# A new order of instructions on every engine of a two-level Strassen-Winograd matmul

## The chip, the core and the metric

The kernel runs on one core of a Trainium2 chip. The metric is device time in microseconds (us) from start to end of one execution, the median of several runs. A core has engines that each work through their own queue of instructions in order: TensorE (PE, matmuls into PSUM), VectorE (DVE), ScalarE (ACT), GpSimd (POOL), and the sync engine's queue (SP), which here issues all DMA transfers. They meet at semaphores: an instruction waits until what it reads has been written, and until what it overwrites has been read.

## What is computed

```python
def setup_inputs():
    B, S, D = 8, 2048, 2048
    return {
        "x": np.random.randn(B, S, D).astype(np.float32),
        "w": np.random.randn(D, D).astype(np.float32),
    }

def reference(x, w):
    cs = np.cumsum(x, axis=1)
    diff = cs - np.concatenate([np.zeros((cs.shape[0], 1, cs.shape[2]), dtype=np.float32), cs[:, :-1, :]], axis=1)
    return np.matmul(diff, w).astype(np.float32)
```

A cumulative sum followed by its differences gives x back, so the work is one matmul: 16384 x 2048 times 2048 x 2048.

## The kernel before, in words

**Tiles.** x is cut into 128 row tiles of 128 x 2048 (1 MB), each loaded as two halves of 512 KB. The first four (`PLAIN = 4`) are multiplied directly in bfloat16 while w, 32 blocks of 512 KB, arrives; these are the `plain.h.r.ko` steps. The other 124 go in groups of four through a Strassen-Winograd scheme in float16, which trades matmuls for sums: a group is two pairs (g and h = g + 2), and from the second group on most products are once more split into seven.

**Stages of a tile** (`role` counts tiles from the group's start). `load` brings a half from memory into one of four staging places. `weigh` (ScalarE, L138) sums its absolute values; `mean` (GpSimd, L157), `scale` (VectorE, L159) and `unit` (GpSimd, L160) turn the sums into a row scale; `narrow` (ScalarE, L170) writes the scaled half as float16; `turn` (SP, L187) is a DMA that transposes it into the place from which TensorE loads it. `load4` to `load7` belong to the next group, `load8` and `load10` to the one after it.

**Products.** `P1`, `P2`, `P5`, `P3` and `P4` are the five products that are split into seven (L554). `P1.0` to `P1.6` are their TensorE steps, four matmuls each; `P1.s1` to `P1.s4` the sums of x that they need (VectorE, `s3` on GpSimd); `in1.Q1`, `in1.Q4`, `in5.t21`, `in3.Q1`, `in3.Q3`, `in4.Q1` sums of w blocks in one shared place `flow` (L520), and `in4.Q3` one that is brought by DMA. Within a product a bank of PSUM is used several times: `P1.first` copies it out after step 0 (ScalarE, L571), `P1.out2` after step 2 and `P1.out4` after step 4, and the step that reuses the bank waits for that copy; `P1.middle` and `P1.last` (VectorE, L520) add the copies in. `S2g T2`, `S2h T2`, `S3g T3`, `S3h T3` are whole products of four steps each (L532).

**Results.** `keep` (ScalarE, L568) scales a bank into one of eight result places, `C11g+P2.g` and the like (VectorE, L579) add further banks, `put` (SP, L587) writes a result out. A result place can be reused by a `keep` only when its `put` has landed.

**Start.** w blocks are cast (`cast w.h.ko`, ScalarE) and their largest value is taken (`max w.h.ko`, VectorE). When all 32 have landed, `max`, `max of all`, `uw` and `uinv` give the scale of w, and `B11`, `B21`, `B12` (VectorE, L415) and `B22` (six on ScalarE, L417) make the float16 blocks of w, eight each. `left over.0` to `.3` (TensorE, L430, 16 matmuls) need B11 and B21. `first x` are quarter loads of the first four tiles, `warm` are matmuls on zeros.

**The order.** The code builds a list of operations with `record(label, engine, ask)`; nothing is issued yet. `emit` sorts the list by a number written out for every label and issues each engine's operations in that order:

```python
        for _, _, engine, ask in sorted(ops, key=when) if places else ops:
            after(engine, ask)
```

where `when` is `period * PERIOD + places[period][label]`, and `places[None]` holds for the periods without a table of their own, 4 to 26. Period 0 is the start with the first group, periods 1 to 30 are the other groups, 31 is the last write. Who computes what, and which buffers are used, is fixed when the list is made; the numbers decide only who stands before whom in each engine's queue. A matmul step, a copy or a sum of one group can so stand among those of the next.

Of the kernel before, what the change touches and what calls it, by code (L numbers as in the profile page):

```python
# [10 lines left out]
def kernel(  # L11
# [33 lines left out]
    PERIOD = 2177  # L45
# [12 lines left out]
    B11, T1, B12, T2, B21, T3, B22, T4 = (  # L58
        [p[:, i // 2, i % 2] for p in pieces] for i in range(8)
    )  # L60
# [4 lines left out]
    uw, uinv, wred = (tiny[:, ds(10 + i, 1)] for i in range(3))  # L65
# [289 lines left out]
    cast = {}  # L355
# [777 lines left out]
    for g in range(PLAIN + 4, END, 4):  # L1133
# [8 lines left out]
            'ones': -4955, 'first x.1.0': -4955, 'numbers': -4941, 'numbers turned': -4926,  # L1142
# [522 lines left out]
```

## Time and profile before

| | us |
|---|---|
| median of 3 runs | 1470.49 (1469.99 to 1476.46) |
| the profiled execution | 1472.2 |
| its span, first to last instruction | 1470.4 |
| TensorE busy in it | 1446.3, 6698 matmuls |
| VectorE busy | 1270.1 |
| ScalarE busy | 1127.1 |
| GpSimd busy | 314.8 |
| transfers of the queue | 366.02 MB, 91.5% of the 16 DMA engines' time |

In the views that follow, a group of instructions is named by its line, engine and operation; `arena<-b` means that it reads PSUM banks and writes the tile `arena`. The time before an instruction in which its engine was idle is put down to the one that released it. A matmul's end is modelled, some 0.16 us after the next one starts, so neighbours overlap and waits look that much shorter.

### The profile page before, as it was taken

What the parts mean: (1) busy time and instruction counts of PE and PEld (TensorE: products, weight loads), DVE (VectorE), ACT (ScalarE), POOL (GpSimd) and SP (SyncE); (2) the same over time, 40 slices, a digit from 0 to 9 for tenths busy, and PEclk for the clock granted to TensorE, in tenths of its full rate; (3) what the DMA queues carried; (4) which work ended last, traced back from release to release, by engine and by line L of the source; (5) the groups of instructions that cost most, each with busy time, mean ns of one, the idle gap of its engine ahead of it and who ended that gap; (6) DMA issues with size and microseconds to landing.
All of it is one profiled execution on the core that took longest, in us unless ns stands there. A gap on an engine that the chain in (4) does not pass through costs nothing.

```text
span 1470.4 us, 20821 instructions
## 1 busy us (share of the span) xinstructions
PE 1446.3 (98%) x6698; PEld 652.4 (44%) x6698; DVE 1270.1 (86%) x2075; ACT 1127.1 (77%) x1742; POOL 314.8 (21%) x400
## 2 busy tenths in 40 slices
PE   8999999999999999999999999999999999999998
PEld 3444444444444444444444444444444444444443
DVE  5998898888889888889888889888889888888887
ACT  5996677877787877777877777877777877787773
POOL 0001122222222222222222222212222212212220
PEclk9999999999999999999999999999999999999999
DMA  9999878999889999889999889999899999988983
GB/s 351 353 261 266 220 212 234 256 265 248 236 251 237 266 264 246 238 253 236 267 263 247 242 244 238 270 264 245 235 254 235 270 263 238 251 243 227 261 215 129
DMA packets 348109, 367.34 MB, mean 250 GB/s; under 512 B 271456, under 2 KB 271456, under 8 KB 348000
## 3 DMA queue, kind: packets, MB, share of 16 engines
q1 hardware_dynamic: 348000, 366.02, 91.5%
q8 instruction: 52, 0.85, 0.3%
q14 instruction: 57, 0.47, 0.1%
HBM read 166.20 MB, written 134.74 MB: 205 GB/s over the span
## 4 chain that ended last, share of the span: by engine, by line
PE 87%; DMA 7%; ACT 3%; DVE 2%; issue 1%; SPq 1%; POOL 0%; DVEq 0%; ACTq 0%; POOLq 0%
PE b L554 54%; PE b L532 30%; DMA F<-in_x_dram 3%; PE b L302 2%; DMA W<-in_w_dram 2%; DMA x<-F 1%; ACT arena L568 1%; ACT F L170 1%; DVE arena L520 1%; ACT waste L138 1%; DVE arena L579 1%; DMA W<-in_x_dram 1%; ACT b L571 0%; DMA out_dram<-arena 0%; ACT arena L571 0%
## 5 line engine op out<-in xcount | busy, mean ns | idle before, releaser
L579 DVE SCALAR_TENSOR_TENSOR arena<-b,tiny,arena 128x512 f32<-128x512 f32 x612 | 444.7, 746 | 85.9 <-ACT arena L568 44.5
L532 PE MATMUL b<-W,x 128*128 128x512 f16 x2176 | 515.9, 379 | 0.0
L554 PEld LDWEIGHTS <-arena 128*128 128x128 f16 x2700 | 263.5, 98 | 330.5 <-issue 15.1
L554 PE MATMUL b<-W,arena 128*128 128x512 f16 x1640 | 399.3, 379 | 3.5 <-ACT b L571 2.1
L568 ACT ACTIVATE arena<-b,tiny 128x512 f32<-128x512 f32 x496 | 321.8, 688 | 46.4 <-PE b L532 18.3
L532 PEld LDWEIGHTS <-x 128*128 128x128 f16 x2176 | 212.7, 98 | 256.9 <-DVE x L520 0.2
L170 ACT ACTIVATE F<-F,tiny 128x1024 f16<-128x1024 f32 x246 | 282.6, 1149 | 47.8 <-DVE tiny L159 45.3
L554 PE MATMUL b<-W,x 128*128 128x512 f16 x1180 | 297.8, 379 | 3.4 <-ACT b L571 2.4
L138 ACT ACTIVATE waste<-F 128x1024 uint8<-128x1024 f32 x246 | 260.4, 1059 | 26.9 <-DMA F<-in_x_dram 25.0
L554 PE MATMUL b<-arena 128*128 128x512 f16 x1060 | 271.1, 379 | 2.5 <-ACT arena L568 1.9
L520 POOL TENSOR_TENSOR arena<-x,x 128x512 f16<-128x512 f16 x118 | 149.1, 1264 | 575.5 <-PE b L554 552.8
L571 ACT COPY arena<-b 128x512 f32<-128x512 f32 x294 | 170.7, 581 | 99.2 <-PE b L554 89.9
L554 PEld LDWEIGHTS <-x 128*128 128x128 f16 x1416 | 138.4, 98 | 173.2 <-issue 6.9
L520 DVE TENSOR_TENSOR b<-b,arena 128x512 f32<-128x512 f32 x294 | 204.0, 694 | 12.8 <-ACT arena L571 12.1
L520 DVE TENSOR_TENSOR arena<-W 128x2048 f16<-128x2048 f16 (+1 forms) x127 | 151.4, 1192 | 11.6 <-PE b L554 11.6
L571 ACT COPY b<-b 128x512 f32<-128x512 f32 x147 | 85.1, 579 | 97.6 <-PE b L554 94.0
L157 POOL TENSOR_SCALAR tiny<-tiny 128x1 f32<-128x1 f32 x124 | 68.3, 551 | 383.6 <-ACT waste L138 358.2
L520 DVE TENSOR_TENSOR x<-x,x 128x1024 f16<-128x1024 f16 x124 | 85.3, 688 | 2.0
L520 DVE TENSOR_TENSOR arena<-W,arena 128x2048 f16<-128x2048 f16 (+1 forms) x70 | 76.0, 1085 | 2.1 <-PE b L554 1.7
L520 DVE TENSOR_TENSOR arena<-x,arena 128x512 f16<-128x512 f16 x118 | 49.8, 422 | 32.2 <-PE b L554 28.8
L160 POOL TENSOR_SCALAR tiny<-tiny 128x1 f32<-128x1 f32 x124 | 63.6, 520 | 2.9
L554 PE MATMUL b<-arena,x 128*128 128x512 f16 x236 | 60.6, 379 | 1.4 <-DMA F<-in_x_dram 1.2
(46 smaller groups left out, 627.3 us busy)
## 6 DMA issues: line engine op xcount, KB each, us to landing
F<-in_x_dram SPq DMA_DIRECT2D x246, 512.0 KB, 5.1
out_dram<-arena SPq DMA_DIRECT2D x240, 512.0 KB, 5.5
W<-in_w_dram SPq DMA_DIRECT2D x32, 512.0 KB, 9.8
arena<-kept SPq DMA_DIRECT2D x29, 512.0 KB, 4.5
out_dram<-arena SPq DMA_DIRECT2D x32, 256.0 KB, 3.2
W<-in_x_dram SPq DMA_DIRECT2D x16, 256.0 KB, 7.8
x<-F SPq DMA_TRANSPOSE x246, 4.5
arena<-in_x_dram SPq DMA_DIRECT2D x2, 512.0 KB, 4.1
```

The source lines that it names most:

```text
L138: lambda: nc.scalar.activation(waste, data, ABS, scale=1.0 / ROW, accum_out=m),
L157: lambda: nc.gpsimd.tensor_scalar(m, m2[:, :1], m2[:, 1:], TINY, ADD, MAX),
L160: record(f"unit{role(t)}", "pool", lambda: nc.gpsimd.tensor_scalar(u, m, uw, None, MUL))
L170: lambda: nc.scalar.activation(to, data, COPY, scale=s),
L302: said = nc.tensor.matmul(to[n], xP[:, r, ko, :], b[:, ds(n * NB, NB)], start=(ko == 0), stop=(ko == KO - 1),)
L520: record(label, engine, lambda: on.tensor_tensor(dst, p, q, op))
L532: said = nc.tensor.matmul(to[n], a[k], b[k][:, n, :], start=(start and k == 0), stop=(k == KH - 1), skip_group_check=True,)
L554: said = nc.tensor.matmul(to, a[k], b[k], start=(start and k == 0), stop=(k == 3), skip_group_check=True)
L568: record(label, "act", lambda: nc.scalar.activation(c, p, COPY, scale=u))
L571: record(label, "act", lambda: nc.scalar.copy(to, p))
L579: label, "dve", lambda: nc.vector.scalar_tensor_tensor(c, p, u, c, MUL, ADD)
```

## The change

The numbers in every table of `places`, and `PERIOD`, are others. The list of operations, their engines, operands and buffers are the same. The core of the diff:

```diff
-    PERIOD = 2177
+    PERIOD = 2168
...
-            'ones': -4955, 'first x.1.0': -4955, 'numbers': -4941, 'numbers turned': -4926,
+            'ones': -4948, 'numbers': -4947, 'numbers turned': -4946, 'zeros': -4945,
+            'first x.0.2': -4944, 'eye': -4909, 'first x.0.3': -4889, 'warm.0': -4870,
+            'w.0.0': -4858, 'warm.1': -4844, 'first x.0.1': -4840, 'first x.0.0': -4835,
...
         None: {
-            'P1.0': -1178, 'P1.first': -1134, 'P4.last': -1128, 'P1.1': -1067, 'C21h+P4.h.0': -1054,
-            'P1.s3': -987, 'P1.2': -951, 'P2.0': -949, 'P1.out2': -948, 'P1.s4': -927,
...
+            'P1.0': -1211, 'P1.first': -1149, 'P1.2': -1064, 'P1.s4': -999, 'P4.last': -994,
+            'P1.1': -983, 'P1.out2': -978, 'P1.s3': -955, 'P2.0': -933, 'C21h+P4.h.1': -911,
```

Sorted, the repeated period (4 to 26) reads as follows; a minus sign marks an operation of the period before.

```
TensorE, before:
P1.0 P1.1 -P4.6 P1.2 P2.0 P1.3 P2.1 P1.4 P2.3 P2.2 P1.5 P1.6 P2.4 P2.5 P5.0 P2.6 S2gT2 S2gT2
S2gT2 P5.3 P5.1 P5.2 S2gT2 P5.4 P5.5 P5.6 S2hT2 S2hT2 P3.1 S2hT2 P3.0 S2hT2 P3.2 P3.3 P3.4 P3.5
P3.6 S3gT3 P4.0 P4.1 S3gT3 S3gT3 S3hT3 P4.2 S3hT3 P4.3 S3gT3 S3hT3 S3hT3 P4.4 P4.5
TensorE, after:
P1.0 -P4.4 -S3hT3 -S3hT3 P1.2 -P4.6 P1.1 P2.0 P1.3 P1.4 P2.3 P2.1 P2.2 P1.5 P2.4 P1.6 P2.5 P2.6
P5.0 S2gT2 S2gT2 P5.3 P5.1 P5.2 S2gT2 P5.4 S2gT2 P5.5 P5.6 S2hT2 S2hT2 S2hT2 P3.1 P3.0 S2hT2
P3.2 P3.3 P3.4 P3.5 P3.6 S3gT3 P4.1 S3gT3 P4.0 S3gT3 S3gT3 P4.2 S3hT3 P4.3 P4.5 S3hT3
ScalarE, before:
P1.first -weigh7.0 -weigh7.1 P1.out2 P2.first -narrow7.0 P1.out4 -narrow7.1 C11g.0 P2.out2
weigh4.0 P2.out4 C11g.1 weigh4.1 C11h.0 narrow4.0 P5.first C11h.1 narrow4.1 weigh6.0 P5.out2
weigh6.1 P5.out4 C22g.0 C12g.1 C22h.0 C22g.1 C12g.0 narrow6.0 C12h.0 narrow6.1 P3.first C22h.1
C12h.1 P3.out2 P3.out4 P4.first weigh5.0 weigh5.1 narrow5.0 narrow5.1 P4.out2 C21g.0 C21h.0
C21g.1 P4.out4 C21h.1
ScalarE, after (C11g.0 and the like are keep C11g.0):
P1.first -C21h.1 -weigh7.0 P1.out2 -weigh7.1 P2.first -narrow7.0 -narrow7.1 C11g.0 P2.out2
P1.out4 C11g.1 P2.out4 weigh4.0 weigh4.1 C11h.0 C11h.1 P5.first narrow4.0 narrow4.1 C22g.0
P5.out2 weigh6.0 P5.out4 weigh6.1 C22g.1 narrow6.0 C12g.1 narrow6.1 C12g.0 C22h.0 C12h.0
P3.first C12h.1 C22h.1 P3.out2 P3.out4 weigh5.0 weigh5.1 narrow5.0 P4.first P4.out2 narrow5.1
C21g.0 C21g.1 C21h.0 P4.out4
VectorE, first third, before:
P4.last -C21g+P4.g.1 -P2.s1 -C21g+P4.g.0 C21h+P4.h.0 P1.s4 -P2.s2 in1.Q4 -scale7 S1g P1.middle
C21h+P4.h.1 P2.s4 S3g P2.middle C11g+P2.g.0 S2g in5.t21 C11g+P2.g.1 P1.last scale4
VectorE, first third, after:
P1.s4 P4.last C21h+P4.h.1 C21h+P4.h.0 -scale7 in1.Q4 P1.middle S1g C11g+P2.g.0 P2.middle P2.s4
P1.last S3g in5.t21 S2g C11g+P2.g.1 scale4
SP, before:
load6.1 put-1.0 put0.0 put2.0 turn4.0 load5.0 load5.1 turn6.0 turn4.1 turn6.1 put0.1 in4.Q3
put2.1 load7.0 load7.1 turn5.0 turn5.1 load8.0 put1.1 put1.0 load8.1 put3.1 turn7.0 turn7.1 load10.0
SP, after:
load6.1 put-1.0 put0.0 put2.0 turn4.0 load5.0 load5.1 turn6.0 turn4.1 turn6.1 put0.1 in4.Q3
put2.1 turn5.0 load7.0 load7.1 turn5.1 put1.0 put1.1 load8.0 load8.1 put3.1 turn7.0 turn7.1 load10.0
```

The parts of the other periods that the prediction speaks of (the number before a colon is the period that an operation belongs to):

```
SP at the start, before: first x.1.0 x.0.0 x.1.1 x.0.3 x.0.1 x.0.2 w.0.2 w.0.0 w.0.1 ...
SP at the start, after:  first x.0.2 x.0.3 w.0.0 first x.0.1 x.0.0 w.0.3 first x.1.1 x.1.0 ...
VectorE after uinv, before: B11.5 B21.1 B11.3 B11.2 B21.0 B11.6 B11.0 B21.2 B21.4 B11.1 scale0
  B11.4 B21.7 B11.7 B21.3 B21.5 B21.6 scale2
VectorE after uinv, after:  B21.3 B21.0 B11.1 B11.7 B12.0 B11.0 B21.6 B11.2 B11.6 B11.3 scale0
  B11.5 B11.4 B21.2 scale2 B21.7 B21.1 B21.5 B21.4
period 1, ScalarE, before: ... weigh6.1 C12g.0 C22g.1 C12h.1 C12h.0 narrow6.0 ...
period 1, ScalarE, after:  ... narrow4.1 C12g.1 C22g.1 weigh6.0 weigh6.1 C12g.0 narrow6.0 ...
period 2, TensorE, before: P2.1 P1.0 P2.0 P1.3 P2.2 P1.2 ...
period 2, TensorE, after:  P1.0 1:S3hT3 1:S3hT3 P2.0 1:P4h.0.1 P2.1 P1.2 P1.3 P2.2 ...
period 2, ScalarE, before: ... weigh4.1 weigh6.0 C11g.1 P1.out4 weigh6.1 C11h.1 ...
period 2, ScalarE, after:  ... weigh4.1 C11g.1 P1.out4 weigh6.0 narrow4.0 C11h.0 ...
period 3, TensorE, before: P1.0 P1.1 2:P4.6 P1.2 P2.0 P1.3 P2.3 ...
period 3, TensorE, after:  P1.0 2:P4.4 2:P4.5 2:S3hT3 P1.1 P1.2 2:P4.6 P2.1 P1.3 P2.0 P1.4 P2.3 ...
period 27, ScalarE, before: ... weigh6.0 P5.first weigh6.1 P5.out2 narrow4.1 ...
period 27, ScalarE, after:  ... P5.first weigh6.0 narrow4.1 P5.out2 weigh6.1 ...
period 28, ScalarE, before: ... C11h.0 narrow4.1 weigh6.0 P5.first C11h.1 ...
period 28, ScalarE, after:  ... C11h.0 weigh4.1 P5.first narrow4.0 weigh6.0 P5.out2 ...
period 29, ScalarE, before: ... C11h.1 weigh4.0 weigh4.1 weigh6.0 P5.first weigh6.1 ...
period 29, ScalarE, after:  ... P2.out4 C11g.1 P5.first weigh4.0 P5.out2 weigh4.1 ...
```

More of the change, by code (lines that the diff above doesn't have):

```diff
@@ L1141 @@
         0: {
-            'ones': -4955, 'first x.1.0': -4955, 'numbers': -4941, 'numbers turned': -4926,
[70 rows of a table removed]
-            'max': -2094, 'weigh0.0': -2088, 'max of all': -2086, 'uw': -2069, 'uinv': -2061,
[77 rows of a table removed]
-        },
[48 rows of a table removed]
-        },
[41 rows of a table removed]
-        },
[41 rows of a table removed]
+            'ones': -4948, 'numbers': -4947, 'numbers turned': -4946, 'zeros': -4945,
[69 rows of a table added]
+            'cast w.1.12': -2142, 'max w.1.12': -2142, 'max': -2076, 'max of all': -2059,
[25 rows of a table added]
+            'B12.5': -1259, 'out': -1248, 'narrow1.0': -1229, 'put out': -1210,
[52 rows of a table added]
+        },
[48 rows of a table added]
+        },
[42 rows of a table added]
+        },
[42 rows of a table added]
         },
         27: {
[41 rows of a table removed]
[41 rows of a table added]
         },
         28: {
[40 rows of a table removed]
[41 rows of a table added]
         },
         29: {
[40 rows of a table removed]
[40 rows of a table added]
         },
         30: {
[32 rows of a table removed]
[32 rows of a table added]
         },
         31: {
-            'P4.last': -1221, 'C21h+P4.h.1': -1110, 'C21h+P4.h.0': -1078, 'put-1.0.1': -1068,
-            'put-1.0.0': -1020,
+            'P4.last': -1181, 'C21h+P4.h.1': -1065, 'C21h+P4.h.0': -1031, 'put-1.0.1': -1021,
+            'put-1.0.0': -989,
         },
         None: {
[41 rows of a table removed]
[40 rows of a table added]
         },
```

931 rows, old and new, of the table places are left out of this document.

## The prediction

> **What bounds the kernel now.** I read the busy lines of the page first, then the stretch table, then what TensorE waited for, and last the order of time around single waits.
>
> ```profile
> PE 1446.3 (98%) x6698; PEld 652.4 (44%) x6698; DVE 1270.1 (86%) x2075; ACT 1127.1 (77%) x1742; POOL 314.8 (21%) x400
> ```
>
> TensorE is busy nearly always, and the change leaves its 6698 matmuls alone, so only the time between them can go. The stretch table (length; for each engine busy us and its instructions; clock; DMA share; GB/s) shows where that time lies:
>
> ```profile
> 0.00:19.54 19.54, 12.52 (x58) 5.69 (x59) 8.58 (x16) 6.63 (x7) 0.19 (x4) 0.91 0.89 309
> 42.00:135.00 93.00, 93.00 (x432) 42.12 (x431) 88.28 (x152) 76.78 (x108) 9.59 (x18) 1.00 0.99 294
> 135.00:300.00 165.00, 158.43 (x724) 70.28 (x723) 139.93 (x240) 120.18 (x187) 37.64 (x43) 1.00 0.88 231
> 300.00:1290.00 990.00, 989.90 (x4577) 447.10 (x4576) 866.48 (x1415) 786.69 (x1235) 230.69 (x291) 1.00 0.94 252
> 1290.00:1430.00 140.00, 135.24 (x621) 60.41 (x619) 117.71 (x191) 104.51 (x166) 33.22 (x41) 1.00 0.87 233
> 1465.50:1470.40 4.90, 0.00 (x0) 0.00 (x0) 1.30 (x2) 0.35 (x1) 0.00 (x0) 0.98 0.59 209
> ```
>
> One step of four matmuls takes 0.864 us when nothing is waited for (the starts 559.13 to 560.86 quoted further down), 0.216 a matmul. Against that rate 135 to 300 lacks 165/0.2157 - 724 = 41 matmuls, 8.8 us; 1290 to 1430 lacks 28, 6.0 us; 300 to 1290 lacks 12.7, 2.7 us over 22 groups. 42 to 135 lacks nothing. With the start and the 4.9 us after the last matmul that is all there is: 17.5 us of waits in three stretches. What ended TensorE's waits (total, times, longest), first for 135 to 300, then for 1290 to the end:
>
> ```profile
> PE b L554 <- ACT b L571: 1.9, 2, 1.4
> PE b L554 <- ACT arena L568: 1.9, 2, 1.1
> PE b L554 <- DMA F<-in_x_dram: 1.2, 1, 1.2
> PE b L532 <- DVE arena L520: 0.7, 1, 0.7
> PE b L554 <- DVE arena L520: 0.4, 1, 0.4
> PE b L554 <- ACT arena L571: 0.2, 1, 0.2
> ...
> PE b L554 <- ACT b L571: 3.0, 4, 1.6
> PE b L554 <- ACT arena L571: 1.3, 2, 1.1
> PE b L554 <- DVE arena L579: 0.4, 1, 0.4
> ```
>
> These sum to 6.3 and 4.7 us, less than 8.8 and 6.0: the ends of matmuls are modelled later than their successors start, so each wait shows some 0.16 short. I scale by 1.4 and 1.28. Most are copies out of PSUM on ScalarE, and what held them is seen at two places (start, length, engine, operation, idle before):
>
> ```profile
> 146.57 1.06 ACT L138 ACTIVATE waste<-F 128x1024 uint8<-128x1024 f32 x1 [0.50 <-DMA F<-in_x_dram]
> 147.62 2.40 ACT L568 ACTIVATE arena<-b,tiny 128x512 f32<-128x512 f32 x4
> 148.92 1.02 PE L554 MATMUL b<-arena 128*128 128x512 f16 x4 [0.80 <-ACT arena L568]
> ...
> 1345.20 1.04 ACT L138 ACTIVATE waste<-F 128x1024 uint8<-128x1024 f32 x1
> 1346.24 0.58 ACT L571 COPY b<-b 128x512 f32<-128x512 f32 x1
> 1346.88 1.02 PE L554 MATMUL b<-W,arena 128*128 128x512 f16 x4 [1.64 <-ACT b L571]
> ```
>
> ScalarE takes its instructions in order. A weigh (L138) stands in the queue for a tile that is still landing, or simply ahead of the copy, and the copy that TensorE needs comes behind it.
>
> **The change, part by part.** Nothing is added or removed; every cost is a matter of who stands behind whom.
>
> *135 to 300 (periods 1 to 4), -5.0.* In period 1 keep C22g.1 now comes before weigh6.0 and weigh6.1, so the wait at 148.92 loses its cause. In period 2 TensorE gets five more steps between P1.0 and P1.3 (two of period 1's S3h T3, its P4h.0.1, then P2.1 and P1.2), 4.3 us, which covers the 1.4 us that the copy P1.first was late; P1.out4 moves ahead of weigh6.0. In period 3 P2.3 moves five steps (4.3 us) back, past the late weigh7.1. I count all of the 1.9 behind L571, half of the 1.9 behind L568 (in period 4 keep C22g.1 still follows weigh6.1, with one TensorE step more of cover), half of the 1.1 behind VectorE and the 0.2 as gone: 3.6 x 1.4 = 5.0. The 1.2 stays: it is keep C11h.0, which still stands ahead of P2.out4. Bounds: 2 to 8.
>
> *1290 to 1430 (periods 27 to 30), -3.0.* In periods 28 and 29 P5.first moves ahead of weigh6.0, in 29 ahead of weigh4.0 too, so of the 3.0 behind L571 the 1.64 quoted and about 0.5 go; in 27 weigh6.1 moves behind P5.out2 and P5.4 behind two more steps, so the 0.3 at P5.4 goes. In 29 narrow5.0 and narrow5.1 still precede keep C21h.1 and P4.out4 (1.1 us), which I leave. 2.4 x 1.28 = 3.0; bounds 1 to 5.
>
> *300 to 1290 (the repeated order), -1.5.* One wait recurs here in every period:
>
> ```profile
> 557.31 1.03 PE L554 MATMUL b<-W,x 128*128 128x512 f16 x4
> 558.17 1.03 PE L532 MATMUL b<-W,x 128*128 128x512 f16 x4
> 559.13 1.02 PE L554 MATMUL b<-W,arena 128*128 128x512 f16 x4
> 559.99 1.03 PE L554 MATMUL b<-W,x 128*128 128x512 f16 x4
> 560.86 1.03 PE L554 MATMUL b<-arena 128*128 128x512 f16 x4
> ...
> 557.43 1.16 ACT L170 ACTIVATE F<-F,tiny 128x1024 f16<-128x1024 f32 x1
> 558.47 0.61 ACT L571 COPY b<-b 128x512 f32<-128x512 f32 x1
> ...
> L138 ACT ACTIVATION_READ_ACCUMULATOR waste<-F 128x1 f32 x246 | 47.5, 193 | 0.0
> ```
>
> P3.0 starts at 557.31, its copy P3.first only at 558.47, right behind narrow6.1; P3.2 follows at 559.13, 0.96 after the step between instead of 0.86. In the new order three short copies stand ahead of P3.first, narrow6.1 before them. By the rows, a weigh or a narrow takes ScalarE 1.05 and a copy 0.5 to 0.58 from one start to the next, and a weigh's sum is out 1.25 after its start (0.19 more, the last row); from P5.4's end P5.out4, weigh6.1 and a wait for mean6 and scale6 make 2.4 us, then two narrows and four copies 4.4: free at 6.8, while eight TensorE steps end at 6.9. I take 0.07 of the 0.10, times 22: 1.5. The rest of the period I walked the same way. P5.first now stands ahead of narrow4.0, with two TensorE steps as cover instead of three, 0.5 us to spare. P2.out2 has one step as cover instead of two; with its copy free to start that suffices, as one step suffices elsewhere in this period. The tightest is VectorE. scale7 now stands early in its queue and holds it until weigh7.1 and mean7 are done. From P1.0's start, the last S3h T3 of the period before ends at 3.7; then come keep C21h.1, weigh7.0, P1.out2 and weigh7.1 (0.58 + 1.05 + 0.5 + 1.25), and mean7: 7.4 us. Behind scale7 stand in1.Q4, P1.middle, S1g, C11g+P2.g.0, P2.middle and more up to S2g, some 7 us of VectorE work with holds for P2.out2 and for P1.6 in it, so that S2g ends at 16.0. Step 19, S2g T2.0.0, starts at 16.4: about 0.3 to spare, if mean7 is short. It can be either:
>
> ```profile
> 535.51 1.52 POOL L157 TENSOR_SCALAR tiny<-tiny 128x1 f32<-128x1 f32 x1 [0.89 <-ACT waste L138]
> 535.74 1.22 DVE L520 TENSOR_TENSOR arena<-W,arena 128x2048 f16<-128x2048 f16 x1
> 545.13 0.30 POOL L157 TENSOR_SCALAR tiny<-tiny 128x1 f32<-128x1 f32 x1 [6.00 <-ACT waste L138]
> ```
>
> The long one ran beside in1.Q4, the short one beside a sum in PSUM. In the new order in1.Q4 stands behind scale7, which waits for mean7, so VectorE is idle then: I take 0.30. At 1.52 P2.4 would be late by about 0.25 a period, 5.5 us in all. Bounds of this part: -2.7 to +5.5.
>
> The Trainium skill, SBUF — State Buffer, "Who interferes with whom", has it that GpSimd and a VectorE instruction with two SBUF inputs exclude each other for a whole instruction; the two rows agree, and by that rule the 5.5 us do not come.
>
> *0 to 135, +0.2.* The first w block is asked for third instead of eighth, so the first real matmuls come earlier; but the transfers fill this stretch (DMA share 0.89, then 0.99), and its end hangs on VectorE:
>
> ```profile
> 63.26 6.72 DVE L415 TENSOR_SCALAR W<-W,tiny 128x1024 f16<-128x1024 f32 x10
> 70.29 4.05 DVE L415 TENSOR_SCALAR W<-W,tiny 128x1024 f16<-128x1024 f32 x6
> 72.01 3.62 PE L430 MATMUL b<-W,arena 128*128 128x512 f16 x16
> ```
>
> The last four of these 16 matmuls start at 74.60 (72.01 + 12 x 0.216), 0.26 after the sixteenth block of B11 and B21 ends (70.29 + 4.05). The new order puts B12.0 among them, so it is the seventeenth: 0.67 later, less 0.26, less what TensorE finds to do meanwhile. Bounds -0.7 (blocks ready sooner) to +1.7, from the clock:
>
> ```profile
> 12.72:16.13 3.41, 1.44 (x6) 0.58 (x6) 1.22 (x1) 2.56 (x3) 0.00 (x0) 1.00 1.03 410
> 16.13:19.54 3.41, 3.41 (x15) 1.75 (x14) 1.70 (x2) 2.79 (x4) 0.00 (x0) 0.50 1.05 408
> ```
>
> After a stretch with TensorE mostly idle the granted clock is 0.50 for 3.41 us, which costs half of it, 1.7. The new order's first matmuls are as gappy, so I expect one such stretch again.
>
> The Trainium skill, TensorE: Matmul & The Clock Gate, "Part 1: The HAM clock gate (the "warmup" mystery)", says the gate judges windows of 3413 ns; the rows agree. By it a second idle window would make the start term +1.9 instead of +0.2.
>
> *New waits, +1.5.* No trace shows the new order's own. Bounds: none, to as much as the old order has in its eight special periods, 8.8 + 6.0 = 14.8. I take a tenth, since the order that repeats (2.7 us in 22 periods) is nearer to what a settled order has.
>
> **Sum:** -5.0 - 3.0 - 1.5 + 0.2 + 1.5 = -7.8. The profiled execution took 1472.2 (span 1470.4), so 1464.4 for it; the median of the runs is 1470.5, 1.7 below, so the forecast is 1462.7.
>
> **The rivals.** *Nearly all waits go:* 1470.5 - 17.5 = 1453. For it: nearly all have one cause, a weigh or a landing ahead of a copy. Against: a write-back's landing and two narrows still stand ahead of copies. *The waits move:* the special periods have as many as before at other places, and only 1.5 to 2 us of the loop are won: 1468.5. For it: VectorE at 88.28 of 93 us in 42 to 135 leaves no room to give. *Slower, by one landing:* put2.1 must have landed before keep C21h.0 reuses its buffer. In the loop put2.1 waits for C12h+Y.1, behind P3.6, which is now TensorE's fortieth step of the period instead of the thirty-seventh; so it goes out some 2.1 us closer to that copy, and the copy stands ahead of P4.out4 and P1.first, which P4.6 and P1.2 wait for.
>
> ```profile
> out_dram<-arena SPq DMA_DIRECT2D x240, 512.0 KB, 5.5
> ...
> 1343.58 0.69 ACT L568 ACTIVATE arena<-b,tiny 128x512 f32<-128x512 f32 x1 [2.12 <-DMA out_dram<-arena]
> ```
>
> The median landing is 5.5 us and about 7 would still do; ScalarE has been held 2.12 by such a landing. If it held TensorE by 0.8 in each of 22 periods, that is +17.6 in place of the loop's -1.5: -6.3 + 17.6 = +11.3, 1481.8. From 0.3 a period on (6.3/22) the kernel is slower than before. Against it: no row shows a wait of this kind between 300 and 1290, and the loads of the loop get more room: weigh6.1 starts about 1 us after load6.1's landing in the old order and, by the same walk, some 3 us after it in the new.
>
> **How the numbers follow.** Forecast 0.49 (own range 1458 to 1467), nearly all waits go 0.20, the waits move 0.18, slower 0.13. A measurement tells 0.5%, 7.4 us, from no change: below 1463.1 is faster, above 1477.8 slower. Over half of the forecast's chance (0.28) and all of the second's are faster: 0.48. The rest of the forecast's and the third's are 0.39 within, and 0.13 slower. The range leaves out half of the slower rival and part of the second: 1454 to 1474.
>
> **What would show it.** Right: between 300 and 1290 TensorE has 4580 or more matmuls in 990 us; 135 to 300 has over 740; no copy behind a weigh that waits for a landing; one stretch at clock 0.50. Wrong: a wait that recurs every 44 us, on keep C21h.0, S2g or P2.out2, or a B block that ends later than 75 us.

## The result, and the profile after

The new order takes 1459.65 us (median of 4 runs, 1458.38 to 1461.24) where the old takes 1471.76 (4 runs, 1469.99 to 1476.46): 0.9913 of the time, with a 95% interval of 0.9887 to 0.994. The forecast was 1462.7. The profiled execution took 1459.5, its span is 1457.7, 12.7 less than before.

The busy lines of the new kernel, and its stretch table (length; for each engine busy us and its instructions; clock; DMA share; GB/s):

```profile
PE 1440.2 (99%) x6692; PEld 652.4 (45%) x6698; DVE 1245.1 (85%) x2075; ACT 1132.1 (78%) x1742; POOL 288.1 (20%) x400
```

```profile
0.00:19.54 19.54, 12.90 (x75) 6.39 (x77) 9.73 (x18) 7.71 (x8) 0.19 (x4) 1.00 0.89 312
42.00:135.00 93.00, 89.49 (x412) 40.15 (x413) 85.52 (x149) 73.81 (x102) 9.04 (x18) 1.00 0.99 289
135.00:300.00 165.00, 164.16 (x759) 74.02 (x758) 143.69 (x249) 125.78 (x196) 35.25 (x45) 1.00 0.89 242
300.00:1290.00 990.00, 989.70 (x4585) 448.39 (x4584) 846.22 (x1418) 793.09 (x1238) 208.28 (x292) 1.00 0.91 251
1290.00:1430.00 140.00, 140.00 (x647) 63.20 (x646) 123.08 (x200) 103.61 (x165) 32.00 (x39) 1.00 0.85 234
1453.00:1457.70 4.70, 0.00 (x0) 0.00 (x0) 0.73 (x2) 0.00 (x0) 0.00 (x0) 0.79 0.59 193
```

Six records of matmuls are missing in this trace, all before 68 us (the weight loads, x6698, are complete). From 135 on the table shows 35, 8 and 26 matmuls more than before in the same stretches. From 42 to 135 it shows 20 fewer, 17 without the missing records: here the new order waits where the old one did not. What ended TensorE's waits between 42 and 135 (total, times, longest), which was an empty list before, then between 135 and 300:

```profile
PE b L532 <- DVE arena L520: 2.3, 1, 2.3
PE b L532 <- DMA x<-F: 0.6, 1, 0.6
PE b L430 <- DVE W L415: 0.5, 1, 0.5
```

```profile
PE b L554 <- ACT arena L571: 0.6, 1, 0.6
PE b L554 <- DVE arena L579: 0.2, 1, 0.2
```

Since both kernels run the same steps, the loss can be set down for each part of the list: the time from a part's first matmul to that of the next part, less its matmuls at 0.2157 us (the rounding of this rate alone is worth 0.2 us in the column 5-26). All kernels of this study in one table (us; "plain" are the bfloat16 steps, "group 0" the first group; the runs behind the first two come below):

| | before the first step | plain | group 0 | groups 1-4 | 5-26 | 27-30 | last step to end | median of runs |
|---|---|---|---|---|---|---|---|---|
| before | 14.4 | 2.7 | 0.0 | 9.3 | 3.2 | 6.6 | 5.3 | 1471.76 |
| after | 12.3 | 2.3 | 4.0 | 1.7 | 0.95 | 1.2 | 6.1 | 1459.65 |
| e1, ten moves on ScalarE | 14.0 | 1.6 | 0.9 | 7.3 | 5.8 | 7.1 | 5.3 | 1471.94 |
| e13, nine of them | 14.6 | 1.3 | 0.0 | 5.7 | 7.5 | 6.0 | 5.4 | 1471.17 |
| e2, old start | 14.7 | 0.6 | 6.6 | 6.1 | 0.95 | 1.2 | 6.0 | 1464.95 |
| e3, old end | 11.8 | 3.1 | 4.0 | 2.0 | 0.95 | 11.1 | 5.3 | 1470.74 |
| e11, old ScalarE, VectorE, GpSimd in 2 and 3 | 11.8 | 1.8 | 5.1 | 23.8 | 0.95 | 1.2 | 5.4 | 1481.20 |
| e9, old transfers | 11.4 | 2.8 | 4.1 | 10.0 | 2.1 | 10.6 | 5.9 | 1479.45 |
| e8, new transfers alone | 14.7 | 2.2 | 0.0 | 11.3 | 53.4 | 15.8 | 6.8 | 1532.98 |
| e6, old order, late load | 14.4 | 1.2 | 0.0 | 9.5 | 49.0 | 7.2 | 5.4 | 1516.19 |
| e12, the same, copy ahead | 15.1 | 1.6 | 0.0 | 9.8 | 49.8 | 6.2 | 5.3 | 1520.05 |
| e7, new order, late load | 11.9 | 2.7 | 5.6 | 2.7 | 12.8 | 1.1 | 6.1 | 1474.41 |
| e5, start mended | 11.6 | 3.3 | 3.5 | 1.9 | 0.95 | 1.5 | 5.9 | 1458.91 |
| e10, writes later | 14.4 | 0.2 | 1.1 | 1.9 | 0.95 | 0.5 | 5.9 | 1457.05 |

Before to after: groups 1 to 4 give 7.5, groups 27 to 30 give 5.5, the repeated order 2.2, the start up to the end of the plain steps 2.5; group 0 costs 3.9 and the end 0.8. But for the medians, each row is one execution. The first two columns differ from one to the next also where the table of period 0 is the same: they sum to 15.3 to 17.1 in the seven traces with the old start (16.2 on average) and to 13.6 to 14.9 in the seven with the new (14.5). The trace of the old order is the slowest of its seven, so of the 2.5 at the start about 1.7 is what these traces give to the order.

### The profile page after: what moved, and what is told of

The parts are those of the page before. It is cut to its first block, busy times and chain, and to the rows that moved or that the text cites. A ratio compares the mean times of both kernels' runs of the same rounds, so it can differ in the third digit from the quotient of the medians.

```text
span 1457.7 us, 20733 instructions
## 1 busy us (share of the span) xinstructions
PE 1440.2 (99%) x6692; PEld 652.4 (45%) x6698; DVE 1245.1 (85%) x2075; ACT 1132.1 (78%) x1742; POOL 288.1 (20%) x400
## 4 chain that ended last, share of the span: by engine, by line
PE 92%; DMA 5%; ACT 1%; issue 1%; DVE 0%; SPq 0%; DVEq 0%; POOL 0%; ACTq 0%
PE b L554 60%; PE b L532 32%; DMA W<-in_w_dram 2%; DMA W<-in_x_dram 2%; DMA out_dram<-arena 0%; DMA x<-arena 0%; DMA F<-in_x_dram 0%; ACT waste L138 0%; ACT arena L287 0%; ACT F L170 0%; DVE arena L579 0%; ACT arena L318 0%; ACT arena L568 0%; ACT W L417 0%; SPq L245 0%
## 5 line engine op out<-in xcount | busy, mean ns | idle before, releaser
L579 DVE SCALAR_TENSOR_TENSOR arena<-b,tiny,arena 128x512 f32<-128x512 f32 x612 | 439.7, 743 | 55.4 <-ACT arena L568 42.8
L554 PEld LDWEIGHTS <-arena 128*128 128x128 f16 x2700 | 264.0, 98 | 321.3 <-issue 3.5
L554 PE MATMUL b<-W,arena 128*128 128x512 f16 x1640 | 405.6, 379 | 0.6 <-ACT arena L571 0.6
L568 ACT ACTIVATE arena<-b,tiny 128x512 f32<-128x512 f32 x496 | 322.3, 685 | 51.4 <-PE b L532 39.4
L554 PE MATMUL b<-W,x 128*128 128x512 f16 x1180 | 297.1, 379 | 0.0
L571 ACT COPY arena<-b 128x512 f32<-128x512 f32 x294 | 169.7, 586 | 147.5 <-PE b L554 136.8
L554 PE MATMUL b<-arena 128*128 128x512 f16 x1060 | 266.9, 379 | 0.5 <-DVE tiny L159 0.3
L520 POOL TENSOR_TENSOR arena<-x,x 128x512 f16<-128x512 f16 x118 | 142.7, 1210 | 543.9 <-PE b L554 511.9
L554 PEld LDWEIGHTS <-x 128*128 128x128 f16 x1416 | 138.5, 98 | 167.4 <-issue 0.7
L157 POOL TENSOR_SCALAR tiny<-tiny 128x1 f32<-128x1 f32 x124 | 41.8, 337 | 439.3 <-ACT waste L138 414.3
L571 ACT COPY b<-b 128x512 f32<-128x512 f32 x147 | 85.0, 578 | 35.8 <-DVE arena L579 20.6
L520 DVE TENSOR_TENSOR x<-x,x 128x1024 f16<-128x1024 f16 x124 | 82.3, 681 | 0.2
L160 POOL TENSOR_SCALAR tiny<-tiny 128x1 f32<-128x1 f32 x124 | 72.1, 583 | 0.7
L554 PE MATMUL b<-arena,x 128*128 128x512 f16 x236 | 60.2, 379 | 0.0
```

Of the source, the lines that this page charges most:

```text
L157: lambda: nc.gpsimd.tensor_scalar(m, m2[:, :1], m2[:, 1:], TINY, ADD, MAX),
L160: record(f"unit{role(t)}", "pool", lambda: nc.gpsimd.tensor_scalar(u, m, uw, None, MUL))
L520: record(label, engine, lambda: on.tensor_tensor(dst, p, q, op))
L554: said = nc.tensor.matmul(to, a[k], b[k], start=(start and k == 0), stop=(k == 3), skip_group_check=True)
L568: record(label, "act", lambda: nc.scalar.activation(c, p, COPY, scale=u))
L571: record(label, "act", lambda: nc.scalar.copy(to, p))
```

## The experiments

**Copies ahead of weighs, nothing else (e1, e13).** The prediction read the waits as copies that stand behind a weigh, a narrow or a keep. So the old order got those moves and no others:

```diff
         1: {
-            'keep C22g.1': -133,
+            'keep C22g.1': -175.5,
         2: {
-            'P1.first': -1015, 'P1.out4': -501,
+            'P1.first': -1018.5, 'P1.out4': -538.5,
         3: {
-            'keep C11h.0': -609,
+            'keep C11h.0': -574.5,
         27: {
-            'weigh6.1': -306,
+            'weigh6.1': -231.5,
         28: {
-            'P2.first': -950, 'weigh6.0': -410,
+            'P2.first': -955.5, 'weigh6.0': -266.5,
         29: {
-            'weigh6.0': -425, 'P4.out4': 994,
+            'weigh6.0': -318.5, 'P4.out4': 918.5,
```

In period 1 keep C22g.1 goes ahead of weigh6.1; in 2 P1.first ahead of weigh4.0 and P1.out4 ahead of keep C11g.1; in 3 keep C11h.0 behind P2.out4; in 27 weigh6.1 behind P5.out2; in 28 P2.first ahead of narrow7.1; in 28 and 29 weigh6.0 behind P5.first; in 29 P4.out4 ahead of narrow5.1.

> The old order, with nine instructions of ScalarE's queue at another place in the special periods (1, 2, 3, 27, 28, 29): each copy out of PSUM that a weigh, a narrow or a keep held up goes ahead of it. TensorE, VectorE and SP keep the old order. Theory (the gain comes from copies that no longer stand behind weighs and landings): each moved copy starts when its bank is ready, so of the waits seen in the old trace about 0.97 (period 1), 1.0 and 0.35 (2), 1.34 (3), 0.42 (27), 0.54 and 1.04 (28), 0.5 and 1.2 (29) go, 7.4 in all: about 1464.5, half of what the new order wins. Rival (the new places of TensorE's steps, which cover the waits, do it): the waits come back at the next copy or at the weigh that is late now, and 2 us at most are won: 1470.

Its run held a tenth move, keep C21h.0 of period 28 behind P1.first of 29, by which that keep reads other values and one part of the result differs. It was run again without it:

> The first run again with the nine moves alone: in that run a tenth was in the kernel, keep C21h.0 of period 28 behind P1.first of 29, so that this keep took the bank after the next product's copy had overwritten it and its part of the output was another. Theory now (a copy moved ahead by itself makes the weigh or keep behind it late, and that is needed as soon): no gain, 1470 to 1474. Rival (the tenth move cost what the nine won): 1466 or less.

Measured: 1471.94, ratio 0.9993 (0.9976 to 1.0009), and 1471.17, ratio 0.9991 (0.9978 to 1.0004). No gain. The stretches of e13:

```profile
135.00:300.00 165.00, 161.86 (x741) 72.14 (x741) 144.47 (x246) 123.22 (x193) 37.83 (x45) 1.00 0.87 238
300.00:1290.00 990.00, 987.02 (x4557) 445.40 (x4556) 864.11 (x1408) 783.84 (x1230) 229.81 (x289) 1.00 0.95 250
1290.00:1430.00 140.00, 136.23 (x623) 60.58 (x622) 118.52 (x192) 104.47 (x166) 33.55 (x41) 1.00 0.86 233
```

By the step starts the named waits did go or shrink (0.97 in period 1, 1.34 in 3 and 1.2 in 29 are gone, 1.8 in 28 is 0.2), and 135 to 300 won 17 matmuls. But others appeared behind what is late now: in 27, where weigh6.1 went back, P5.1 and P5.6 lose 1.3 where P5.4 had lost 0.4; in 28 P2.4 and P5.4 lose 1.5 and in 30 P1.2 loses 0.5, where nothing was lost before. So 1290 to 1430 comes to no more than 623 (621 before). And 300 to 1290, whose order was not touched, has 20 matmuls fewer than in the first trace: late loads, of which that trace had none. One of them (start, length, engine, operation, idle before):

```profile
945.56 1.06 ACT L138 ACTIVATE waste<-F 128x1024 uint8<-128x1024 f32 x1 [1.14 <-DMA F<-in_x_dram]
...
946.61 0.57 ACT L571 COPY arena<-b 128x512 f32<-128x512 f32 x1
...
947.23 1.02 PE L554 MATMUL b<-W,arena 128*128 128x512 f16 x4 [0.85 <-ACT arena L571]
```

weigh6.1 waits for its tile, the copy P5.out4 stands behind it, and P5.6 waits for the copy. There are four such waits at P5.6 in groups 5 to 26 of e13 and two in e1, which has the same lists up to group 27, so their number differs from one execution to the next. From one trace each it can't be told whether the moves in periods 1 to 3 add to them. What the runs show is that the sum is no gain: the 4.2 us that e13's trace wins in groups 1 to 4 and 27 to 30 are lost again in between.

**The end and the start put back (e3, e2).** Each is the new kernel with tables from the old: in e3 those of periods 27 to 31, in e2 that of period 0, in which one number is fitted so that a keep still comes ahead of the product that reuses its bank (the diff is e2's).

```diff
         0: {
-            'ones': -4948, 'numbers': -4947, 'numbers turned': -4946, 'zeros': -4945,
+            'ones': -4955, 'first x.1.0': -4955, 'numbers': -4941, 'numbers turned': -4926,
...
-            'keep C21.1#2': 1040,
+            'keep C21.1#2': 1273.5,
...
```

> The new order, with the old tables for periods 27 to 31. Theory: the gain of the end belongs to the order of the end, so the 5.6 us between 1290 and 1430 come back, near P5.2 of 28 and 29 and P4.6 of 29: 1465. Rival: the end is better because the repeated order hands it its loads and banks earlier: 1460 to 1461, and 1290 to 1430 stays near 645 matmuls.

> The new order, with the old table for period 0 (the start and the first group). Theory: the new start is the one part that lost. By 135 us TensorE had done 621 matmuls in the old order and 615 in the new (609 records and the 6 that are missing), 6 x 0.216 = 1.3 us behind, so with the old start about 1458.4, no wait of 2.4 us near 91, and 0 to 19.54 slow again. Rival: the seam between the old start and the new period 1 costs as much as the old start wins, or the new start is better because the blocks of w are ready 1.9 us earlier: 1460 to 1462.

Measured: e3 1470.74, 11.1 more than the new order (9.7 by the spans), twice what was expected. Its stretch from 1290 on:

```profile
1290.00:1430.00 140.00, 135.53 (x623) 60.45 (x622) 118.07 (x191) 105.51 (x166) 31.64 (x39) 1.00 0.85 233
```

623 matmuls in place of 647 are 5.2 us, so the loss of the old end comes back with the old tables. Most of the rest lies at the seam: between 1275 and 1290 P1.1, P1.4 and P5.0 of period 27 lose 4.7 us, which the old order does not lose there. I read it as the new group 26 handing over in another state than the old group 27 was written for; no run tests that.

e2: 1464.95, 5.3 more; theory and size were wrong. Group 0 itself lost 6.6: 3.1 in one wait and 2.9 in the four steps behind it, which ran at half the clock. Stretches of e2 around that wait:

```profile
105.89:109.30 3.41, 1.29 (x6) 0.49 (x5) 1.25 (x4) 0.62 (x2) 0.00 (x0) 1.00 1.00 143
109.30:112.71 3.41, 2.58 (x7) 0.91 (x7) 3.38 (x9) 3.38 (x5) 0.00 (x0) 0.50 0.47 141
112.71:116.13 3.42, 3.42 (x10) 1.18 (x9) 3.39 (x9) 1.88 (x5) 0.72 (x1) 0.50 1.12 276
```

Groups 1 to 4 lose 4.4 us more behind the old start than behind the new. That is the seam of which the rival spoke, at more than its price. So a table put beside a neighbour that it was not written for costs something at the seam, and neither e2 nor e3 prices a table by itself.

**One kind of queue alone (e8, e9, e11).** The five lists of all orders obey the same dependences, so lists of two orders can be joined where no two of them wait for each other in a circle, as SP's list can with the other four. The core of the edit, for e8 in the old kernel (`others` holds the new numbers of SP) and for e9 in the new (there it holds the old ones):

```diff
     def emit(places=None):
-        def when(op):
-            at, label = op[:2]
-            own = places[at] if at in places else places[None]
+        def number(op):
+            at, label, engine = op[:3]
+            tables = others if engine == "sp" and at > 0 else places
+            own = tables[at] if at in tables else tables[None]
             return at * PERIOD + own.get(label, 0)
...
```

> The old order on TensorE, ScalarE, VectorE and GpSimd, and SP's transfers from period 1 on in the new order. Theory (the gain lies in the order of the engines' instructions, since SP's list is nearly the same): no gain, 1470 to 1476. Rival (the loads and write-backs land earlier because SP asks for them in a better order): 1466 or less, with fewer loads that land under 0.2 us ahead of their weigh in periods 1 to 4 (10 of 31 in the old trace, 6 in the new).

> The new order on TensorE, ScalarE, VectorE and GpSimd, and SP's transfers from period 1 on in the old order. Theory: nearly all of the gain stays, 1460 to 1464; SP waits now and then for an input that comes later in the new order. Rival (the transfers' order makes the gain): 1468 or more.

Measured: 1532.98, ratio 1.0401 (1.0371 to 1.0432), and 1479.45, ratio 1.0046 (1.003 to 1.0063). Both theories fell: the transfers' order alone does not gain, and the engines' order without it does not either. The two have to fit. In e9 the stretches show where:

```profile
135.00:300.00 165.00, 158.42 (x720) 70.54 (x719) 137.85 (x239) 120.79 (x189) 33.89 (x43) 0.99 0.85 229
300.00:1290.00 990.00, 988.87 (x4580) 447.85 (x4579) 844.91 (x1415) 789.29 (x1232) 209.46 (x293) 1.00 0.91 251
1290.00:1430.00 140.00, 132.98 (x604) 59.18 (x603) 114.26 (x184) 101.04 (x159) 29.13 (x35) 0.99 0.85 227
```

In the repeated order, where SP's two lists differ in the places of turn5.0, load8.0, put1.0 and put1.1, the old list is nearly as good for the new engines (4580); the new list for the old engines costs some 50 us there (e8). In the special groups all is lost and more, in a few long waits (3.8 at P1.2 of 2, 5.0 at P5.2 of 28). Behind each TensorE lost 1.4 more in a stretch at half the clock (178.54 to 181.96 and 1349.32 to 1352.73). In both, ScalarE stood still for a landing, that of load8.0 ahead of weigh4.0 of period 2 and that of put3.1 ahead of keep C11h.1 of 28 (L713 is L568 here, moved down by the lines added above it):

```profile
174.88 1.06 ACT L138 ACTIVATE waste<-F 128x1024 uint8<-128x1024 f32 x1 [3.79 <-DMA F<-in_x_dram]
...
1345.16 0.69 ACT L713 ACTIVATE arena<-b,tiny 128x512 f32<-128x512 f32 x1 [5.25 <-DMA out_dram<-arena]
```

The last of the three is the new kernel in which TensorE and SP keep the new order in periods 2 and 3, and ScalarE, VectorE and GpSimd have the old (`engine in ("act", "dve", "pool") and at in (2, 3)` in the line above):

> The new order, but in periods 2 and 3 ScalarE, VectorE and GpSimd keep the old order; TensorE and SP have the new one. Theory (TensorE's steps cover only what the copies and sums of the same order leave to cover; no engine's order is worth anything alone): 135 to 300 falls from 759 matmuls to 735 or fewer, 5 us or more: 1465 or more. Rival (TensorE's five steps more between P1.0 and P1.3 are cover enough): under 1.5 us lost: 1460 to 1461.

Measured: 1481.20, ratio 1.0058 (1.004 to 1.0076), 21.6 more than the new order. TensorE's waits between 100 and 300 (L699 and L716 are L554 and L571 here, moved down by the lines added above them):

```profile
PE b L699 <- ACT b L716: 7.8, 4, 4.8
PE b L699 <- DVE b L665: 3.2, 1, 3.2
PE b L699 <- ACT arena L716: 2.2, 4, 1.2
```

The steps that were to cover late copies do not cover them when the copies come in the old order. Direction as expected, size four times it. Not all of the 21.6 is missing cover: the old lists meet the new ones at two seams, and TensorE runs at half the clock from 225.86 to 232.69 and from 287.30 to 290.72 (at most half of that time is lost by it, an estimate of up to 5.1 us).

**Late landings (e6, e7, e12).** One transfer of the repeated order is made late in both kernels by the same edit:

```diff
         None: {
...
-            'load6.1': -567,
+            'load6.1': -405.5,
...
```

(In the new kernel from -541 to -404.5. In both it then stands behind put-1.0 and put0.0.)

> The old order, with load6.1 of the repeated period (4 to 26) behind put-1.0 and put0.0 instead of ahead of them. In the old trace that makes it go out 1.4 us later; it lands 0.9 and 0.6 us ahead of weigh6.1 (periods 12 and 18), so it would be 0.4 to 0.8 us late, and P5.out4 and scale6 stand right behind weigh6.1. Theory (what the new order has won is room for landings): TensorE loses that in nearly every of 23 periods, 9 to 17 us: 1482 to 1490. Rival (the waits are only a matter of a few places in the special periods): the write-backs now go out earlier by as much, and the loss is under 5 us: under 1478.

> The new order with the same edit: load6.1 of the repeated period behind put-1.0 and put0.0. In the new trace put0.0 goes out at 16.7 of the period, so load6.1 goes out 1.6 to 2.2 us later, more than in the old order; it landed 1.6 to 2.6 us ahead of weigh6.1. Theory (room for landings): it still lands in time or some tenths late, 1460 to 1463, and 300 to 1290 keeps over 4575 matmuls. Rival (the new order has no more room than the old): as much as in the old order, 9 to 17 us: 1469 to 1477.

Measured: e6 1516.19, ratio 1.0292 (1.0269 to 1.0314), 44 us more than the old order; e7 1474.41, 14.8 more than the new. Row of the repeated order, e6 and then e7:

```profile
300.00:1290.00 990.00, 954.69 (x4374) 427.74 (x4373) 835.16 (x1350) 751.82 (x1179) 229.49 (x279) 1.00 0.92 240
```

```profile
300.00:1290.00 990.00, 983.32 (x4533) 441.73 (x4531) 831.08 (x1397) 782.92 (x1219) 185.90 (x287) 1.00 0.91 248
```

Over groups 5 to 25 one period, 44.13 us long in the old order (one of 44.40), grew to between 44.5 and 48.2; in the new, 44.04 long, to between 44.04 and 46.33. The theory held in its ranking, and both sizes were too small. I had counted how much later the load goes out (1.4 us; in e6 it is 1.0 on average over these groups). It lands 2.7 later on average (1.1 to 4.7), since it is now third in a row of three transfers, and such a row lands in order, one each 1.27 us (18.28, 19.57 and 20.82 after P1.0 in period 10 of the old trace).

The new order has more room for this. There load6.1 goes out 14.3 to 16.6 after P1.0 and lands 0.7 to 3.4 ahead of weigh6.1 (2.2 on average), which starts at 23.13; in the old it goes out 12.1 to 14.6 after P1.0 and lands 0.1 to 2.9 ahead (1.1 on average) of a weigh6.1 at 19.68. Over the same groups the places of 32 of 168 writes were used again less than 1 us after the write had landed in the old trace, and of 8 in the new.

Is it then the copy behind the weigh? In the new order P5.out4 stands ahead of weigh6.1; e12 does that to e6, where load6.1 stays late:

```diff
         None: {
...
-            'weigh6.1': -163,
+            'weigh6.1': -91.5,
...
```

> The old order with the late load6.1 (behind put-1.0 and put0.0, 2.0 us a period lost), and in the same repeated period weigh6.1 behind P5.out4, as in the new order. Theory: of the 2.0 us the 1.2 to 1.7 at P5.6 are the copy that stands behind the weigh that waits for the landing; with the copy ahead weigh6.1 still starts at the landing, but one copy (0.57) fewer follows it up to P3.first, so P3.2 is 1.1 to 1.2 late in place of 2.0 in all: about 1496. Rival (the loss is the chain weigh6.1, scale6, narrow6.1, P3.first, whoever stands ahead): 1512 or more.

Measured: 1520.05, no better than e6. TensorE's waits between 300 and 1290, e6 and then e12:

```profile
PE b L554 <- ACT arena L571: 28.6, 21, 2.6
PE b L554 <- ACT arena L568: 4.8, 18, 0.5
```

```profile
PE b L554 <- ACT arena L568: 36.6, 21, 2.3
```

The 21 waits for the copy are gone, and 21 waits for a keep, at P3.1, have taken their place. The rival was right that the chain from weigh6.1 over mean6 and scale6 to the keeps, narrows and copies behind scale6 sets the loss, whoever stands ahead. But what makes weigh6.1 late is another thing than in e6. There it waits for its load in each of groups 5 to 25. In e12 it starts straight behind the copy in 17 of these 21 groups, at 21.40 after P1.0, when its load has landed; period 12 (start, length, operation, idle before):

```profile
655.27 0.58 ACT L571 COPY arena<-b 128x512 f32<-128x512 f32 x1 [1.14 <-PE b L554]
655.75 1.06 ACT L138 ACTIVATE waste<-F 128x1024 uint8<-128x1024 f32 x1
```

The copy itself waits for the matmuls of P5.4 until 20.92, 1.24 after the 19.68 at which weigh6.1 starts in the old order. So in the old order weigh6.1 has room on neither side: behind the late load it is late, and behind the copy it is as late (2.1 us a group) without any landing. The move by itself only exchanges one cause for another.

**The new waits of group 0 (e5, e10).** The wait of 2.3 us near 91 in the new kernel is S1g on VectorE, and S1g waited for a transposing transfer (timeline of the new kernel, start, length, operation, idle before):

```profile
90.20 0.69 DVE L520 TENSOR_TENSOR arena<-x,x 128x1024 f16<-128x1024 f16 x1 [1.38 <-DMA x<-arena]
...
90.95 1.25 PE L532 MATMUL b<-W,arena 128*128 128x512 f16 x5 [2.27 <-DVE arena L520]
```

The time from issue to landing of such transfers between 80 and 92, before and then after:

```profile
DMA to landing us min/median/max: 3.3/4.4/4.9
```

```profile
DMA to landing us min/median/max: 6.2/6.8/7.2
```

In the new order turn1.0 stands behind load3.0, load3.1 and one write, turn1.1 behind two writes more. e5 moves those three writes behind both, and four other operations as its expectation says:

```diff
         0: {
-            'put out': -1210, 'put out.1.1.1': -1090, 'put out.1.3.0': -1043,
+            'put out': -1039.7, 'put out.1.1.1': -1039.6, 'put out.1.3.0': -1039.5,
-            'keep C11g.0': -942, 'keep C11g.1': -895,
+            'keep C11g.0': -995.5, 'keep C11g.1': -995.4,
-            'T1.3': -826, 'A11h B11.0.1': -1077,
+            'T1.3': -906.5, 'A11h B11.0.1': -1085.5,
```

> The new order, with seven numbers of period 0 changed: the three writes put out, put out.1.1.1 and put out.1.3.0 go behind turn1.1, both keep C11g go ahead of weigh3.0, T1.3 ahead of C11g+V.0, and one TensorE step (A11h B11.0.1) ahead of one that waits for turn2.1. Theory: the 2.43 us wait near 91 is turn1.0 and turn1.1, which took 7.21 and 6.17 us to land behind two loads and three writes (4.90 and 4.39 in the old order); they land 3 us earlier and the 2.43 and the 0.73 at 80.9 go: 1456.5. Rival: the 16 transfer engines are busy 99% of this stretch, so the same bytes land at the same time, and the writes or loads that now come later hold something else: 1459 to 1461.

Measured: 1458.91, ratio 0.9902 (0.9882 to 0.9923). The rival was right: turn1.0 and turn1.1 landed at 86.8 and 87.6 in place of 87.6 and 90.2, so the waits of 0.7 and 2.4 shrank to 0.1 and 0.9, but S1h T1.1.0 now loses 1.5 at 99.5 for turn3.1, which stands behind two loads and the writes. e10 takes the writes behind that too, since the trace shows that their places are used again only 8 to 33 us after they land:

```diff
         0: {
-            'put out.1.0.1': -910, 'load4.0': -976, 'load4.1': -949,
+            'put out.1.0.1': -1039.8, 'load4.0': -1039.7, 'load4.1': -1039.6,
-            'put out.1.1.0': -641, 'put out.1.1.1': -1090, 'put out.1.3.1': -909,
+            'put out.1.1.0': -614.9, 'put out.1.1.1': -614.8, 'put out.1.3.1': -614.7,
-            'put out.1.3.0': -1043, 'put out': -1210,
+            'put out.1.3.0': -417.9, 'put out': -417.8,
...
         2: {
-            'C21g+P4.g.1': 1184,
+            'C21g+P4.g.1': 1119.5,
         27: {
-            'C21h+P4.h.0': -919,
+            'C21h+P4.h.0': -946.5,
```

The loads of group 1 and put out.1.0.1, which S1h waits for, now follow turn1.1; the writes follow turn3.1, two of them load6.1.

> The new order with fourteen numbers changed. In period 0 the writes put out, put out.1.1.1, put out.1.3.0, put out.1.3.1 and put out.1.1.0, whose places are needed only 8 to 30 us later, go behind turn1.1, load4.0, load4.1, turn3.0 and turn3.1, which were used the moment they landed; the four other changes of the mended start stay. At two more places a sum that a product waits for goes ahead on VectorE: C21g+P4.g.1 of period 2 (0.40 and 0.7 lost near 219 and 227) and C21h+P4.h.0 of period 27 (0.47 near 1279). Theory (a landing is late by the transfers that stand ahead of it in the queue): the 3.8 us of waits between 42 and 135 fall under 1.5, and about 1 us goes behind 135: 1456. Rival (the engines for transfers are full, so the waits move on to the next landing): 1459 to 1460, as with the start mended before.

Measured: 1457.05 (5 runs, 1455.28 to 1459.25), ratio 0.9892 (0.9873 to 0.991). TensorE's waits between 42 and 135, the landing of the transposing transfers between 80 and 92 (here turn1.1, turn3.0 and turn3.1), and the stretch:

```profile
PE b L532 <- ACT arena L568: 0.7, 1, 0.7
```

```profile
DMA to landing us min/median/max: 3.2/3.2/5.1
```

```profile
42.00:135.00 93.00, 92.30 (x428) 41.55 (x426) 86.92 (x152) 74.64 (x104) 10.86 (x18) 1.00 1.02 298
```

The waits did not move on, although the share of the transfer engines stays at 1.0. turn1.0 and turn1.1 took 4.9 and 4.4 us to land in the old order, 7.2 and 6.2 in the new, 6.9 and 6.4 in e5, and 5.8 and 5.1 in e10; turn3.0 and turn3.1, with the writes behind them, took 3.2 each. The landings were late by what stood ahead of them. Group 0 loses 1.1 in place of 4.0. In period 3 the sum moved ahead only shifted the loss from P2.1 to P2.3; in 27 the 0.47 went. e10 has the shortest median of all kernels here. Its interval overlaps that of the new order, so by the times alone it isn't told from it; the trace shows the 2.8 us.

## Why the prediction was right, and where it was not

The sum came out: -12.7 in the profiled span where -7.8 was forecast, and the time lies 3.1 below the forecast, inside its own range. That it came so near is in part luck: four terms gave 8.4 us more than forecast, and two cost 3.2 more. By terms:

- **135 to 300, -5.0 and bounds to -8:** -7.5. Right in place and sign, a third too small: the wait for keep C11h.0 that was counted as staying (1.2 x 1.4) went too, as put3.1 had landed 4 us before that keep's turn; another write, put1.0, holds P2.out2 of period 3 for 0.7.
- **1290 to 1430, -3.0 and bounds to -5:** -5.5, past the bound. The two narrows ahead of P4.out4 that I left standing cost nothing in the new order: P4.4 ends 3.4 us after the second of them.
- **The repeated order, -1.5:** -2.2 in the one pair of traces. The recurring 0.10 at P3.2 went altogether. What the prediction didn't have is that the old order's loss differs from one execution to the next: its 3.2 came without late loads, while e1 and e13, with the same list in groups 5 to 26, lost 5.8 and 7.5 with them. The new list lost 0.95 in each of six executions (after, e2, e3, e5, e10, e11).
- **The start, +0.2:** -2.5 up to the end of the plain steps, of which some 1.7 are left over the seven traces of each start. The step that failed is "The new order puts B12.0 among them, so it is the seventeenth: 0.67 later". B12.0 does stand there, but the blocks begin earlier, which the prediction held only as a bound (-0.7): w's last block lands at 58.6 in place of 60.3, and uinv, which frees all B blocks, comes 2.1 earlier, so the last block that left over.3 needs ends at 73.1 in place of 74.3. The half-clock stretch that was expected didn't come here (1.00 in the first row of the stretch table). e10 has it again (0.91 there), and so have five of the seven traces with the old start, so whether it hangs on the order or on the execution stays open.
- **New waits, +1.5:** +3.9, all in group 0. I looked for them among the special periods, and they lie in the stretch that had been free of waits, behind writes that were put ahead of transposing transfers.
- **The end:** +0.8, not foreseen; the last result's chain after the last matmul is that much longer.

One open point, mean7 at 0.30 or 1.52 us, fell as it was taken. The group of mean before and after (busy, mean ns, idle before); in groups 4 to 25 mean7 took 1.3 to 1.6 us in the old trace and takes 0.30 in the new:

```profile
L157 POOL TENSOR_SCALAR tiny<-tiny 128x1 f32<-128x1 f32 x124 | 68.3, 551 | 383.6 <-ACT waste L138 358.2
L157 POOL TENSOR_SCALAR tiny<-tiny 128x1 f32<-128x1 f32 x124 | 41.8, 337 | 439.3 <-ACT waste L138 414.3
```

One way of reasoning failed though its sum came out: each wait was priced by itself, as if a copy that moves ahead of a weigh were a gain. "The wait at 148.92 loses its cause" held as far as it goes, since in e13 the 0.97 in period 1 are gone by that move alone. But nine such moves together gain nothing in time (0.9991): in 27 and 28 the weigh that goes back feeds the next wait, and in e12 the weigh behind the copy is late in every group. TensorE's added cover without the lists that belong to it costs 21.6 in e11, seams and half clock included. None of the orders that mix old and new lists of the engines gains; what each single move brings is not shown.

The slower rival had put2.1 land closer to keep C21h.0. The opposite happened: the keep stands later in ScalarE's queue as well, and the room grew from 0.4 to 1.3 us on average over groups 5 to 25 (from 0.1 to 0.9 up to 0.5 to 1.9). It had moved one side of the distance only. "Nearly all waits go" was nearer to the truth from 135 on: of 19.0 lost in groups 1 to 30, 3.8 are left.

Why the new lists have room just there is not shown; only that they leave more time between a landing and its use.

## What to carry to other kernels

Where engines work through fixed queues, a wait that one move removes can come back at the next link of the same chain, unless the other engines' queues and the transfers give that link room: count the chain from the transfer to the matmul, not the instruction that the profile names. In a list of transfers put those whose landing is awaited ahead of those whose place is not needed for some time; on the single queue of this kernel a transfer landed behind all that were asked for ahead of it. And compare several executions before a loop is called free of waits: the old order, whose load6.1 lands as little as 0.1 us ahead of its use, shows its late landings only now and then.

## What was not expected of the hardware

**Rows of transfers.** The three transfers of 512 KB above land in the order of issue, 1.29 and 1.25 us apart, so a place in the list is worth more than the time of issue. In each of the 14 traces all 846 transfers of SP's queue land in the order in which they are issued. The Trainium skill, DMA: Bandwidth & Descriptors, "Queues, rings and completion order", has it that each of the 16 engines takes its descriptors in the order of the ring, and that completion need not keep that order; here the landings did.

**SP held by a transposing transfer.** Two such issues between 80 and 92, old order and then new (shortest, median and longest ns on SP):

```profile
L187 SPq DMA_TRANSPOSE x<-arena x2: 1237/1814/2391, 80.9 to 82.2; - x2
```

```profile
L187 SPq DMA_TRANSPOSE x<-arena x2: 2372/2746/3120, 80.4 to 84.0; - x2
```

With loads and writes in flight SP itself is held up to 3.1 us, and all that it has to issue next with it (4.4 in e5).

**The clock.** A wait of 3.1 us halved the clock in e2 for what came next (the rows above: 1.29 of 3.41 us busy, then 0.50 for two stretches). A wait of as long at 91 in e3 didn't:

```profile
86.37:89.78 3.41, 1.96 (x10) 0.69 (x7) 1.88 (x4) 3.38 (x6) 1.26 (x4) 1.00 1.23 282
89.78:93.20 3.42, 1.94 (x9) 0.90 (x10) 2.66 (x5) 2.18 (x2) 0.00 (x0) 1.00 0.94 314
```

There the idle time fell into two windows, and neither was mostly idle. The Trainium skill, TensorE: Matmul & The Clock Gate, "Part 1: The HAM clock gate (the "warmup" mystery)", says that the windows run freely, 3413 ns each; both cases agree with that, and the same wait can cost 3 us more or nothing by where it falls. In all 14 traces the clock changes only at whole multiples of 3.413 us from its first change, and the rows above lie on that grid. Up to the last matmul 20 windows at full clock were followed by one at half. TensorE was busy for at most 1.50 us in each of them, and for 1.51 or more in all but one (1.36, in e6) of the windows that were not.
